# Keys of three heads beside the small columns: summed tile by tile of the tokens, on all eight PSUM banks

## The chip, the cores and the metric

The kernel runs on one core of a Trainium2 chip. The metric is the device time of one execution in microseconds; shown is the median of several runs. The engines are TensorE (PE, matrix products into PSUM), VectorE (DVE), ScalarE (ACT) and GpSimd (POOL); SyncE (SP) issues most of the transfers. PSUM has eight banks of 512 fp32 values on each of 128 partitions.

## The reference, cut to what matters

The block is a hybrid decoder layer on 16 + 512 = 528 tokens of width 1024. Only its head matters for the change:

```python
n = _rmsnorm(h, pre_mix_norm[l])
proj = jnp.einsum('btd,dn->btn', n, w_in[l])
(gq, gk, gv, gz, gb, ga, aq, ak, av, iq, ik, iw, gate_a, gate_b) = jnp.split(proj, split_at, axis=-1)
y_gdn = _gdn_branch(gq, gk, gv, gz, gb, ga, ...)   # causal convolution, silu, gated delta rule
y_dsa = _dsa_branch(aq, ak, av, iq, ik, iw, ...)   # sparse attention
```

`gk` has eight heads of 128 columns. `gb`, `ga`, `ik` and `iw` are 8, 8, 64 and 8 columns, 88 in all; the kernel calls them misc. From `gb` and `ga` come the write strength and the decay of the delta rule, without which its inverse (I + L)^-1 cannot begin.

## The kernel before, in words

Every fp32 product is done in three: an operand is split into a high part (a copy in the matmul's reduced fp32 form) and a low part (the rest), and hi·hi, hi·lo and lo·hi are summed. `wload` loads a chunk of weights (`raw`, 2 buffers), makes `hi` on ACT and `lo` on DVE (`hl`, 5 buffers).

The input comes transposed, as eight tiles of 128 features by 528 tokens. The first loop (lines 131 to 142) loads tile k to `xr`, makes `nhi` on ACT and `nlo` on DVE, squares it and adds the square to `sqs`. The norm itself (one factor per token) is applied after the products, because it commutes with them.

`proj_a` (line 184) multiplies one chunk of weights, held as the stationary operand, with all tokens: two halves of 264 tokens, for each half the eight tiles k, three products each. A chunk is thus 48 products into two PSUM tiles. It is called for misc (88 columns, line 203) and then for each head of the keys (`keys`, line 321), later for values and queries.

`token_scales` (line 144) sums `sqs` over the features with five products by a vector of ones (`ssn`), takes the inverse root (`rn`) and spreads it over the partitions (`rb`, via the matrix `ones` and diagonal matrices). misc is transposed by tokens (`scp`), scaled to `sc`, and yields the decay `gg`, its running sums `gcp` (with the triangle `tri`), and through memory the matrix `E`. `conv` scales a head's columns by `rb` (line 297), convolves them with four taps (ACT line 298, DVE line 301) and applies silu. `key_norms` sums the squares (`kss`), `products` makes L of four heads at a time (`gp`, `lhs`), and 31 steps on DVE (`substitute`) invert its blocks of 32, whose results go to `Y` and into the products `pm`.

PSUM tiles come from two pools: `pp`, 3 banks, for the long sums, and `sp`, 5 banks, for the rest. Buffers named `cv` and `y` (two of each) hold a head's columns, for heads 2, 3, 6 and 7 a wide buffer `tb` (two; the first one holds `tri` and `ones` until `gcp`).

The program's order is not the engines' order: a planner puts each engine's instructions in order from its own estimate of when they are ready, with the program's order as priority; `tc.issue_after(x)` asks that what follows stands behind x on its engine. On the chip each engine then takes its instructions strictly in that order.

Of the kernel before, what the change touches and what calls it, by code (L numbers as in the profile page):

```python
# [10 lines left out]
F32 = mybir.dt.float32  # L11
F32R = mybir.dt.float32r
# [7 lines left out]
P = 128  # L20
# [13 lines left out]
IDX_D = 64  # L34
S4 = {"a": 4 * T, "b": 4 * L}
# [3 lines left out]
def hybrid_block(ctx: ExitStack, tc: tile.TileContext, io: dict):  # L39
# [29 lines left out]
    # ---------------------------------------------------------------- constants  # L69
# [19 lines left out]
    # ---------------------------------------------------------------- weights  # L89
    def wload(src, n, name, spare=False):  # L90
        """one chunk of weights, split; spare: in the buffers tb and st"""
# [11 lines left out]
    def rsqrt(out, a, shape, tag):  # L103
        """out = a ** -0.5 (a > 0): Newton steps from a guess by the exponent"""
# [19 lines left out]
    # ---------------------------------------------------------------- normed activations, transposed and split  # L124
# [5 lines left out]
    sq = [slots.tile([P, 4096], F32, tag=("s5", "s6")[x], name=f"sq{x}")[:, : 4 * T].rearrange("p (k t) -> p k t", t=T) for x in range(2)]  # L130
    for k in range(KT):
        nc.sync.dma_start(xr[:, k, :], io["hT"][:, k, :])
        if k == 0:
            w_misc = wload(io["w_misc"], 8 * 88, "misc")
# [6 lines left out]
        if k:  # L141
            V.tensor_tensor(sqs, sqs if k > 1 else sq[0][:, 0, :], sq[k // 4][:, k % 4, :], ALU.add)

    def token_scales():
        """1 / rms of the tokens: on partitions (rn) and along the free axis on every partition (rb)"""
# [26 lines left out]
    # ---------------------------------------------------------------- dense products, weights stationary  # L172
    marks, todo = [], []

    def later(keep=0, part=None):
        """what the tensor engine does with earlier convolved columns, behind a part of the latest products"""
        while len(todo) > keep:
            if part is None:
                todo.pop(0)()
            else:  # L180
                with tc.issue_after(marks[part].ins):
                    todo.pop(0)()

    def proj_a(w, name, moving=None, m=P, full=True):
        """columns of one weight chunk [P, 8, m] against the tokens: psum parts [(tile, first column, n)]"""
# [14 lines left out]
    # ---------------------------------------------------------------- small columns: index key, beta, decay, index weights  # L200
    misc = const("misc", [96, T])
    G.memset(misc[64:96, :], 0.0)
    for pt, c, n in proj_a(w_misc, "misc", m=88):
        S.copy(misc[:88, c : c + n], pt[:88, :n])
# [36 lines left out]
    # cumulated log decay in each chunk (the 16 leading tokens, then chunks of 128)  # L241
# [16 lines left out]
    # rows of gc, through memory, on every partition  # L258
# [10 lines left out]
    # decay between the tokens of a chunk: E[p, (h j), f] = exp(-|gc_p - gc_f|)  # L269
# [14 lines left out]
    # ---------------------------------------------------------------- causal convolution and silu  # L284
    silu = []

    def conv(g, c0, parts_of, out, name, wide=False):
        """out = silu(conv) of the tokens from c0"""
        if wide:
            both = wk.tile([P, 2, T], F32, tag="tb", name=f"cb_{name}", bufs=2)  # L290
            cv, y = both[:, 0, :], both[:, 1, : T - c0]
        else:
            cv = wk.tile([P, T], F32, tag="cv", name=f"cv_{name}", bufs=2)
            y = wk.tile([P, T], F32, tag="y", name=f"cy_{name}", bufs=2)[:, : T - c0]
# [11 lines left out]
    # ---------------------------------------------------------------- keys of the delta rule  # L306
# [10 lines left out]
    # XL: blocks 0, 1 (and below them) and 2 of the inverse; XL, L1: the blocks of L below the diagonal of 64 and of 32  # L317
# [3 lines left out]
    def keys(h):  # L321
        w = wload(io["w_k"][h], 1024, f"k{h}")
        parts = proj_a(w, f"k{h}")
        later(1, 0)
        sq = conv(8 + h, 0, parts, kT[:, h, :], f"k{h}", wide=h % 4 > 1)
        S.activation(sq, kT[:, h, :], AF.Square)
        todo.append(lambda: key_norms(h, sq))
# [10 lines left out]
    def products(x):  # L338
        """L[c, s] = beta_c r_c^2 (k_c . k_s) E of 4 heads (i = h * 4 + j); its blocks on the diagonal, by memory, to lanes"""
# [23 lines left out]
        # lane = x * 64 + i * 4 + block  # L363
# [20 lines left out]
    # ---------------------------------------------------------------- (I + L)^-1: 32-blocks, one on each lane  # L384
# [5 lines left out]
    def substitute(nlane, n, lt, x, tmp):  # L390
        """x = (I + L)^-1 of the block of each lane, then its transpose in tmp; in steps"""
# [42 lines left out]
    # ---------------------------------------------------------------- values of the delta rule: r beta v, tokens on partitions  # L434
    vb = slots.tile([P, 32, P], F32, tag="s5", name="vb")
    vbm = cst.tile([NM, NH, P], F32, tag="st", name="vbm", bufs=2)
    for h in range(NH):
# [4 lines left out]
        if h == 1:  # L442
# [3 lines left out]
            # upper triangle (with the diagonal) of E for the scores  # L446
# [14 lines left out]
    # ---------------------------------------------------------------- queries; scores against the keys of the chunk  # L461
# [32 lines left out]
    # ---------------------------------------------------------------- dense products, tokens stationary  # L494
    def rows_part(pt, pairs, lhs, t, cs, first=True, last=True):
        """adds to one psum tile the products of some chunks [P, 2, 512], (number, (hi, lo)), for the columns cs"""
# [9 lines left out]
    def proj_half(src, name, lhs, evac):  # L506
        """512 columns for all tokens, chunk by chunk of the weights"""
# [724 lines left out]
```

## Time and profile before

| | us |
|---|---|
| median of 3 runs (lowest, highest) | 1077.09 (1076.67, 1077.24) |
| span of the profiled execution, first to last instruction | 1075.6 |
| what lies around that span, against the median | 1.5 |
| PE busy in the span | 1054.0 |
| PE busy in its first 20 us | 9.95 |

A timeline row reads: start, time, engine, line, operation, output <- inputs, shapes, how many; in brackets, how long the engine had been idle and what ended that. Matmuls are pipelined: their rows overlap, and what one costs is the step from one start to the next. An fp32 product that is not split (of the identity, of keys with keys) appears as two matmul rows.

### The profile page before, as it was taken

The page shows a single profiled execution, that of the slowest core. Times are in us where ns is not written, and L with a number is a line of the kernel's source. Part 1 is how long each engine was busy: PE and PEld are TensorE (multiplying, and loading weights), DVE is VectorE, ACT ScalarE, POOL GpSimd, SP SyncE. Part 2 cuts the span into 40 slices and gives each one's busy share as a digit, 9 for nine tenths or more (in the row PEclk, how much of TensorE's full clock was granted, in tenths as well). Part 3 has the DMA queues.
Part 4 walks back from the last instruction along what each step waited for, and adds up shares of the span by engine and source line. Part 5 has one row for each costly group of instructions (what it writes and reads, how often), then busy time and mean ns, then how long its engine had stood idle before and what let it go on. Part 6 is the DMA issues. An engine that isn't in the chain of part 4 may idle for free.

```text
span 1075.6 us, 15893 instructions
## 1 busy us (share of the span) xinstructions
PE 1054.0 (98%) x6249; PEld 903.8 (84%) x6249; DVE 682.8 (63%) x1502; ACT 461.4 (43%) x854; POOL 61.6 (6%) x85
## 2 busy tenths in 40 slices
PE   6999999999999999999999999999999999999996
PEld 5999999999997678898888888898888888888885
DVE  5797899516689789957867555695442343343346
ACT  5465555444268432235665432473432332232130
POOL 4202302100000000000000000000000000000022
PEclk9999999998999999999999999999999999999999
DMA  5433424210133022232121235332322333333332
GB/s 177 117 102 108 116 82 136 68 41 2 43 101 115 20 79 80 97 99 82 56 59 59 80 90 187 96 95 83 98 88 90 97 98 98 87 90 98 98 98 79
DMA packets 28235, 96.44 MB, mean 90 GB/s; under 512 B 3632, under 2 KB 3968, under 8 KB 28160
## 3 DMA queue, kind: packets, MB, share of 16 engines
q1 hardware_dynamic: 25440, 87.51, 26.1%
q0 software_dynamic: 2720, 7.92, 2.8%
q8 instruction: 49, 0.80, 0.3%
q14 instruction: 26, 0.21, 0.1%
HBM read 90.14 MB, written 5.28 MB: 89 GB/s over the span
## 4 chain that ended last, share of the span: by engine, by line
PE 89%; DVE 6%; DMA 2%; ACT 2%; issue 1%; SPq 0%; DVEq 0%; ACTq 0%
PE up L1102 5%; PE up L1103 5%; PE up L1101 5%; PE d L503 4%; PE d L504 4%; PE d L502 4%; PE pa_dense L889 2%; PE pa_dense L890 2%; PE pa_dense L888 2%; PE pa_bg L194 1%; PE pa_q L195 1%; PE pa_q L193 1%; PE pa_q L194 1%; PE pa_bg L193 1%; PE pa_bg L195 1%; PE bd L1009 1%
## 5 line engine op out<-in xcount | busy, mean ns | idle before, releaser
L1102 PE MATMUL up<-n2l,hi_up 128*128 128x512 f32 (+1 forms) x288 | 106.8, 372 | 0.0
L1101 PE MATMUL up<-n2h,hi_up 128*128 128x512 f32 (+1 forms) x288 | 106.6, 371 | 0.0
L1103 PE MATMUL up<-n2h,lo_up 128*128 128x512 f32 (+1 forms) x288 | 106.6, 371 | 0.0
L100 DVE TENSOR_TENSOR lo_up<-raw_up,hi_up 128x1024 fp32r<-128x1024 f32 x32 | 39.2, 1225 | 71.0 <-PE up L1102 53.0
L100 DVE TENSOR_TENSOR lo_d<-raw_d,hi_d 128x1024 fp32r<-128x1024 f32 x24 | 29.4, 1226 | 78.4 <-PE d L503 56.0
L502 PE MATMUL d<-hi_d,uh 128*128 128x512 f32 x192 | 75.9, 396 | 0.0
L504 PE MATMUL d<-hi_d,ul 128*128 128x512 f32 x192 | 75.9, 395 | 0.0
L503 PE MATMUL d<-lo_d,uh 128*128 128x512 f32 x192 | 75.9, 395 | 0.0
L1102 PEld LDWEIGHTS up<-n2l,hi_up 128*128 128x128 f32 x288 | 54.2, 188 | 10.3
L1101 PEld LDWEIGHTS up<-n2h,hi_up 128*128 128x128 f32 x288 | 54.2, 188 | 10.3
L1103 PEld LDWEIGHTS up<-n2h,lo_up 128*128 128x128 f32 x288 | 54.1, 188 | 10.3
L1105 ACT ACTIVATE rup<-up 128x512 f32<-128x512 f32 (+1 forms) x36 | 19.9, 552 | 99.6 <-PE up L1103 99.6
L99 ACT CAST hi_d<-raw_d 128x1024 fp32r<-128x1024 f32 x24 | 25.2, 1049 | 59.6 <-PE d L504 59.6
L99 ACT CAST hi_up<-raw_up 128x1024 fp32r<-128x1024 f32 x32 | 33.4, 1044 | 24.0 <-PE d L504 22.7
L504 PEld LDWEIGHTS d<-hi_d,ul 128*128 128x128 f32 x192 | 36.1, 188 | 8.7
L502 PEld LDWEIGHTS d<-hi_d,uh 128*128 128x128 f32 x192 | 36.1, 188 | 8.7
L503 PEld LDWEIGHTS d<-lo_d,uh 128*128 128x128 f32 x192 | 36.1, 188 | 8.7
L888 PE MATMUL pa_dense<-nhi,hi_dense 128*128 128x512 f32 x96 | 39.3, 409 | 0.0
L889 PE MATMUL pa_dense<-nlo,hi_dense 128*128 128x512 f32 x96 | 38.0, 396 | 0.0
L890 PE MATMUL pa_dense<-nhi,lo_dense 128*128 128x512 f32 x96 | 38.0, 396 | 0.0
L546 PE MATMUL pb_z<-hi_z,nhi 128*128 128x256 f32 x128 | 37.9, 296 | 0.0
L193 PE MATMUL pa_k<-nhi,hi_k 128*128 128x264 f32 x128 | 37.1, 290 | 0.0
(570 smaller groups left out, 3079.3 us busy)
## 6 DMA issues: line engine op xcount, KB each, us to landing
raw_up<-w_up SPq DMA_DIRECT2D x32, 512.0 KB, 3.6
raw_d<-w_down SPq DMA_DIRECT2D x24, 512.0 KB, 3.6
raw_k<-w_k SPq DMA_DIRECT2D x8, 512.0 KB, 4.1
raw_v<-w_v SPq DMA_DIRECT2D x8, 512.0 KB, 4.2
raw_q<-w_q SPq DMA_DIRECT2D x8, 512.0 KB, 3.5
raw_z<-w_z SPq DMA_DIRECT2D x8, 512.0 KB, 3.6
raw_w_ga<-w_ga SPq DMA_DIRECT2D x8, 512.0 KB, 3.6
raw_bg<-w_bg SPq DMA_DIRECT2D x8, 512.0 KB, 3.6
```

The lines of the kernel that those rows point to most:

```text
L99: S.copy(hi[:, :n], raw[:, :n])
L100: V.tensor_tensor(lo[:, :n], raw[:, :n], f(hi[:, :n]), ALU.subtract)
L193: TE.matmul(pt[:m, :n], hi[:, ws], mh[:, k, ms], start=(k == 0), stop=False)
L502: TE.matmul(pt, lh, whi, start=beg, stop=False)
L503: TE.matmul(pt, lh, wlo, start=False, stop=False)
L504: TE.matmul(pt, ll, whi, start=False, stop=end)
L888: TE.matmul(pt, hi[:, ws], nhi[:, k, NM:], start=(k == 0), stop=False)
L889: TE.matmul(pt, hi[:, ws], nlo[:, k, NM:], start=False, stop=False)
L890: mm = TE.matmul(pt, lo[:, ws], nhi[:, k, NM:], start=False, stop=(k == KT - 1))
L1101: TE.matmul(pt, hi[:, ws], n2h[:, k, ms], start=(k == 0), stop=False)
L1102: TE.matmul(pt, hi[:, ws], n2l[:, k, ms], start=False, stop=False)
L1103: TE.matmul(pt, lo[:, ws], n2h[:, k, ms], start=False, stop=(k == KT - 1))
```

## The change

The eight tiles are still loaded in order, but the weights of misc and of key heads 0, 1 and 2 now come with them, for two tiles at a time (944 columns: 2 x 88 and 3 x 2 x 128), and each tile's products go at once into eight PSUM tiles that stay open over all k: misc, k0, k1, k2, two halves each. Ahead of them stand 20 products of the identity with itself, into a bank that the sums later overwrite. After the eighth tile the sums are copied to SBUF, and `keys` of heads 0 to 2 starts from these copies. Comments are dropped; nothing else differs.

```diff
+NHEAD = 3
+    heads = [(88 * 2 * (i > 0) + 256 * max(i - 1, 0), 88 if i == 0 else P) for i in range(NHEAD + 1)]
+    hps = [[ptile(f"hd{i}{x}", pp if i > 1 and i + x != 4 else sp) for x in range(2)] for i in range(NHEAD + 1)]
+    for _ in range(20):
+        warm = TE.matmul(hps[NHEAD][1][:, :P], ident, ident, start=True, stop=True)
+    def head_weights(k):
+        n = 2 * 88 + 256 * NHEAD
+        raw = wp.tile([P, 1024], F32, tag="raw", name=f"raw_head{k}", bufs=2)
+        nc.sync.dma_start(raw[:, : 2 * 88], io["w_misc"][:, k * 88 : (k + 2) * 88])
+        nc.sync.dma_start(raw[:, 2 * 88 : n].rearrange("p (h c) -> p h c", h=NHEAD), io["w_k"][:NHEAD, :, k * P : (k + 2) * P].rearrange("h p c -> p h c"))
+        hi, lo = (wp.tile([P, 1024], F32R, tag="hl", name=f"{x}_head{k}", bufs=5) for x in ("hi", "lo"))
+        S.copy(hi[:, :n], raw[:, :n])
+        V.tensor_tensor(lo[:, :n], raw[:, :n], f(hi[:, :n]), ALU.subtract)
+        return hi, lo
     for k in range(KT):
         nc.sync.dma_start(xr[:, k, :], io["hT"][:, k, :])
-        if k == 0:
-            w_misc = wload(io["w_misc"], 8 * 88, "misc")
+        if k % 2 == 0:
+            hw = head_weights(k)
...
+        for (o, m), pts in zip(heads, hps):
+            ws = slice(o + k % 2 * m, o + k % 2 * m + m)
+            for x in range(2):
+                ms = slice(x * HT, x * HT + HT)
+                with tc.issue_after(warm.ins):
+                    TE.matmul(pts[x][:m, :HT], hw[0][:, ws], nhi[:, k, ms], start=(k == 0), stop=False)
+                    TE.matmul(pts[x][:m, :HT], hw[0][:, ws], nlo[:, k, ms], start=False, stop=False)
+                    TE.matmul(pts[x][:m, :HT], hw[1][:, ws], nhi[:, k, ms], start=False, stop=(k == KT - 1))
...
-    for pt, c, n in proj_a(w_misc, "misc", m=88):
-        S.copy(misc[:88, c : c + n], pt[:88, :n])
+    for x in range(2):
+        S.copy(misc[:88, x * HT : x * HT + HT], hps[0][x][:88, :HT])
+    headc = []
+    for i in range(NHEAD):
+        headc.append(conv_columns(f"k{i}", wide=i % 4 > 1))
+        for x in range(2):
+            (S.copy if x else V.tensor_copy)(headc[i][0][:, x * HT : x * HT + HT], hps[1 + i][x][:, :HT])
...
     def keys(h):
-        w = wload(io["w_k"][h], 1024, f"k{h}")
-        parts = proj_a(w, f"k{h}")
-        later(1, 0)
-        sq = conv(8 + h, 0, parts, kT[:, h, :], f"k{h}", wide=h % 4 > 1)
+        if h < NHEAD:
+            sq = conv(8 + h, 0, [], kT[:, h, :], f"k{h}", columns=headc[h])
+        else:
+            parts = proj_a(wload(io["w_k"][h], 1024, f"k{h}"), f"k{h}")
+            later(1, 0)
+            sq = conv(8 + h, 0, parts, kT[:, h, :], f"k{h}", wide=h % 4 > 1)
         S.activation(sq, kT[:, h, :], AF.Square)
         todo.append(lambda: key_norms(h, sq))
```

`conv_columns` is the allocation of `cv` and `y` (or the wide buffer), taken out of `conv`; `HT` is 264, `KT` 8.

## Rows read from the trace of the kernel before

**Rows 1.** The page's first part: the span, and PE's busy time, share and instructions.
```profile
span 1075.6 us, 15893 instructions
PE 1054.0 (98%) x6249; PEld 903.8 (84%) x6249; DVE 682.8 (63%) x1502; ACT 461.4 (43%) x854; POOL 61.6 (6%) x85
```

**Rows 2.** The waits of PE over the whole span: waiting line, whom it waited for, us in total, times, longest.
```profile
PE pa_misc L193 <- ACT hi_misc L99: 6.6, 1, 6.6
PE pa_misc L193 <- ACT nhi L135: 2.4, 1, 2.4
PE pa_misc L194 <- DVE nlo L136: 1.0, 1, 1.0
PE vtp L453 <- ACT cy_v L303: 0.9, 1, 0.9
PE vtp L453 <- DVE lhs L360: 0.8, 1, 0.8
```

**Rows 3.** Stretches of the span: length, busy time of PE, PEld, DVE, ACT, POOL, then granted clock, DMA share and GB/s.
```profile
0.00:20.00 20.00, 9.95 (x50) 8.86 (x50) 11.42 (x15) 11.37 (x19) 11.79 (x26) 1.00 0.58 185
9.00:13.00 4.00, 1.59 (x6) 1.25 (x6) 2.62 (x2) 3.38 (x6) 2.40 (x3) 1.00 1.04 407
29.85:83.80 53.95, 53.79 (x441) 51.88 (x440) 45.24 (x108) 29.00 (x63) 7.57 (x11) 1.00 0.41 118
83.80:121.90 38.10, 36.45 (x314) 35.52 (x313) 29.38 (x75) 22.47 (x47) 14.48 (x14) 1.00 0.44 123
```

**Rows 4.** The timeline of PE at the start, matmuls only.
```profile
11.93 0.52 PE L194 MATMUL pa_misc<-nlo,hi_misc 128*88 128x264 f32 x1 [1.00 <-DVE nlo L136]
...
16.82 0.42 PE L193 MATMUL pa_misc<-nhi,hi_misc 128*88 128x264 f32 x1
17.04 0.42 PE L195 MATMUL pa_misc<-nhi,lo_misc 128*88 128x264 f32 x1
...
17.62 0.28 PE L195 MATMUL pa_misc<-nhi,lo_misc 128*88 128x264 f32 x1
...
26.41 0.28 PE L193 MATMUL pa_k<-nhi,hi_k 128*128 128x264 f32 x1
...
30.07 0.29 PE L193 MATMUL pa_k<-nhi,hi_k 128*128 128x264 f32 x1
```

**Rows 5.** PE's groups by form from 0 to 43.3 us: line, operation, shapes, count | busy us, mean ns | idle before.
```profile
L193 PE MATMUL pa_k<-nhi,hi_k 128*128 128x264 f32 x49 | 14.4, 294 | 0.0
...
L164 PE MATMUL pb<-dg,tri 128*128 128x128 f32 x8 | 1.6, 290 | 0.0
L152 PE MATMUL ssn<-one,sqs 128*128 128x1 f32 x8 | 1.1, 253 | 0.0
L208 PE MATMUL scp<-ident,misc 32*128 32x32 f32 x4 | 0.6, 233 | 0.0
L246 PE MATMUL gcp<-gg,tri 128*128 128x32 f32 x2 | 0.4, 286 | 0.0
L244 PE MATMUL gcp<-gg,tri 128*128 128x32 f32 x2 | 0.4, 286 | 0.1
...
```

**Rows 6.** The timelines of ACT and DVE at the start.
```profile
5.73 0.78 ACT L99 CAST hi_misc<-raw_misc 128x704 fp32r<-128x704 f32 x1
9.62 0.73 ACT L135 ACTIVATE nhi<-xr,gT 128x528 fp32r<-128x528 f32 x1 [3.11 <-DMA xr<-hT]
24.18 0.38 ACT L296 COPY cv_k<-pa_k 128x264 f32<-128x264 f32 x1 [2.75 <-PE pa_k L195]
...
10.38 5.02 DVE L136 SCALAR_TENSOR_TENSOR nlo<-xr,gT,nhi 128x528 fp32r<-128x528 f32 x5 [2.95 <-ACT nhi L135]
18.54 1.22 DVE L100 TENSOR_TENSOR lo_k<-raw_k,hi_k 128x1024 fp32r<-128x1024 f32 x1
22.60 2.19 DVE L142 TENSOR_TENSOR sqs<-sqs,sq 128x528 f32<-128x528 f32 x3
```

**Rows 7.** The timeline of POOL: the identity is made; the eight transfers to `E` are issued.
```profile
1.22 0.29 POOL L72 TENSOR_SCALAR_AFFINE_SELECT ident<-ident 128x128 f32<-128x128 f32 x1
...
44.67 6.01 POOL L272 DMA_DIRECT2D E<-gcd x8 [2.19 <-DMA gcd<-gts]
```

**Rows 8.** Transfers issued from 0 to 130 us: out<-in, queue, count, KB each, median us from issue to landing.
```profile
xr<-hT SPq DMA_DIRECT2D x8, 264.0 KB, 7.6
E<-gcd POOLq DMA_DIRECT2D x8, 256.0 KB, 6.7
raw_misc<-w_misc SPq DMA_DIRECT2D x1, 352.0 KB, 4.0
```

**Rows 9.** The timelines of PE and DVE: the token scales and the running sums of the decay.
```profile
25.16 1.19 PE L152 MATMUL ssn<-one,sqs 128*16 128x1 f32 x10
29.68 0.17 DVE L116 SCALAR_TENSOR_TENSOR rn<-t_n,y_n 128x5 f32<-128x5 f32 x1
39.13 0.20 PE L247 MATMUL gcp<-gg,tri 16*16 16x8 f32 x2
```

**Rows 10.** The chain that ended last, from 0 to 210 us: products of keys with keys, 16 of them in 32 matmuls.
```profile
79.50 3.68 PE gp L358 x32
```

**Rows 11.** The timelines of POOL and PE: the last transfer into Y, and the first product that reads Y.
```profile
191.09 0.65 POOL L417 DMA_DIRECT2D Yb<-yd  x1
210.69 2.11 PE L582 MATMUL pm<-Ya,lam 32*32 32x32 f32 x64
```

More of the change, by code (lines that the diff above doesn't have):

```diff
@@ L198, in proj_a, with conv_columns @@
         return parts
+    def conv_columns(name, wide=False):
+        if wide:
+            both = wk.tile([P, 2, T], F32, tag="tb", name=f"cb_{name}", bufs=2)
+            return both[:, 0, :], both[:, 1, :]
+        return [wk.tile([P, T], F32, tag=x, name=f"{x}_{name}", bufs=2) for x in ("cv", "y")]
     misc = const("misc", [96, T])
     G.memset(misc[64:96, :], 0.0)
-    for pt, c, n in proj_a(w_misc, "misc", m=88):
-        S.copy(misc[:88, c : c + n], pt[:88, :n])
+    for x in range(2):
[5 more added lines that the diff above has]
+            (S.copy if x else V.tensor_copy)(headc[i][0][:, x * HT : x * HT + HT], hps[1 + i][x][:, :HT])
     scp = stile("scp")
@@ L285, in hybrid_block, with conv @@
     silu = []
[L287 to L294, printed above, removed]
+    def conv(g, c0, parts_of, out, name, wide=False, columns=None):
+        cv, y = columns or conv_columns(name, wide)
+        y = y[:, : T - c0]
         for pt, c, n in parts_of:
```

## The prediction

> **What bounds the kernel now.** I read the page's first part first: PE is busy 1054.0 of 1075.6 us [rows 1], so only time in which PE stands or runs slowly can be won. PE's waits come next [rows 2]: of 11.7 us in the five rows, 10.0 lie in the products of misc, at the very start; the other two, 0.9 and 0.8 us at the transposes of the values (`vtp`), are the next place where PE stands. The stretches agree: in the first 20 us PE is busy 9.95 [rows 3]. Then the timeline of PE, for what "busy" hides [rows 4]: consecutive misc products start 0.22 us apart at 16.82 and 17.04, while key products of the same length take 30 steps from 26.41 to 30.07, 0.122 us each; the row at 17.62 already has the shorter duration (0.28 against 0.42). Half the pace: PE ran at the lower of its two levels (1.2 GHz) until about 17.5 us and at 2.4 GHz from there. The granted-clock column reads 1.00 for the whole stretch [rows 3], so here I go by the steps. Before the rise PE had worked without a long pause from 11.93.
>
> How much is lost? Misc and heads 0 to 2 are 4 x 48 = 192 products. Up to 43.3 us the grouped view counts 49 of each of the three key products, 147 in all, 144 of which belong to heads 0 to 2 [rows 5]; so these 192 end at about 43.2. At the fast pace they are 192 x 0.122 = 23.4 us. In the same stretch PE also does the small work: the five groups shown after the keys are 4.1 us busy [rows 5], seven still smaller ones of 0.2 to 0.4 bring them to 5.8, and since neighbours overlap I take 5.3. Lost: 43.2 - 23.4 - 5.3 = 14.5 us. A later start of PE's useful work, or a shorter one, moves the end one for one, as long as PE is kept fed later.
>
> **The change part by part.**
>
> *The identity products.* 20 fp32 products are 40 matmuls. At the fast level such a matmul costs 3.68 / 32 = 0.115 us [rows 10]; slow I scale by 0.22 / 0.122 to 0.21. The identity is finished at 1.22 + 0.29 = 1.5 us [rows 7], so they run from about 1.6. All fast would end at 6.2, all slow at 10.0. Between the two I take 27 slow and 13 fast, 1.6 + 5.7 + 1.5 = 8.8: nearer to all slow, because the misc products after a rest were slow for most of their run [rows 4]. PE has nothing else to do until 6.6 [rows 2], so the first 5 us cost nothing.
>
> *The first weights.* One load of 352 KB took 4.0 us to land [rows 8]; now it is 472 KB in two transfers: scaled, 5.4 us from an issue at 1.7, 7.1, and the cast (944 columns against 704 in 0.78 us [rows 6], 1.0) gives 8.1, hidden behind the identity products. If it takes the 7.6 us of the tokens' tiles [rows 8], it lands at 9.3 and PE starts at 10.3, 1.5 us later. So PE starts at 8.8, bounds 8.1 and 10.3.
>
> *Keeping PE fed.* A tile now brings 24 products, 2.9 us fast. Tile 1 was split at 9.62 [rows 6]; with more ahead of it I allow 11. PE reaches it at 8.8 + 2.9 = 11.7. Bytes are the same as before, 4 x 472 = 352 + 3 x 512 KB. The new pieces are shorter (704 and 1024 bytes a row), which no load of [rows 8] shows as such. The nearest are the eight transfers to `E`, rows of 512 bytes: 2.1 MB issued over 6.0 us [rows 7], the last landing some 6.7 later [rows 8], about 165 GB/s; the loads of 9 to 13 us move 407 GB/s [rows 3]. At those ends all tiles and weights, 4.1 MB, are in by 27 and by 12 us; the last tile is needed at 8.8 + 7 x 2.9 = 29. On SP the loads of tiles 5 to 7 now stand behind two loads that wait for a `raw` buffer, freed when the first and second `lo` are made, about 9.5 and 14: no one is late by that. ACT and DVE cast as many columns as before (3776), only earlier: 1.0 and 1.1 us four times. DVE's list until the last `nlo` is 8 x 1.0 + 4 x 1.1 [rows 6], 12.4, with the adds of `sqs` (0.73 each) 17.5: done at 24 at the latest, before PE needs it. Cost nothing, and 2 to 3 us if PE has to wait for each of the first tiles.
>
> *The end of the sums.* 8.8 + 23.4 = 32.2 us. Lost is then 8.8 instead of 14.5: **gain 5.7 us**; with the bounds of the start 4.2 to 6.4.
>
> *The copies out.* All eight banks are open, so nothing else on PE can run until one is copied. Misc is summed first within a tile, and its copies (0.38 [rows 6]) are done while the heads' last products run; the first `pp` bank is free some 0.5 us after its last product, while the last bank is still summed. Nothing, at most 1 us. Under Matmuls, "Perfetto Trace Analysis" of the Trainium skill says independent groups should rotate through different banks, so that copying one out overlaps the next group's products. By that rule this change gives up the overlap; the trace has no stretch with eight banks open that could show its price.
>
> *What becomes late.* `ssn` needs a bank of `sp`, and those five are held until the misc copies at about 30.5 (29.2 for the last tile's start, 0.7 of misc, a copy). It ran at 25.16 and will run at 31 to 33. `rn` followed its start by 4.5 us, 1.2 of it another head's `lo`; it was ready at 29.85 and is now at 34.4 to 36, so 4.6 to 6.1 us later, and `rb`, `gcp` [rows 9], `E` and the inverse with it. Heads 0 to 2 wait in SBUF for `rb`. Head 3's wide buffer is the one that holds `tri` until `gcp`, which goes from 39 to about 44; PE then has three `pp` banks for heads 3 and 4, and head 4's second half comes due at 45: 0 to 1.5 us. DVE worked 45.2 of 53.95 us from `rn` to the end of the keys' convolutions (83.8) [rows 3]. Two `lo` (2.4 us [rows 6]) are now made before `rn`, leaving 42.8. Without a pause it ends at 77.2, with half of its old 8.7 us of pauses, from 34.4, at 81.6: 2.2 us earlier than before, where PE is 5.7 earlier. The difference, 3.5, must come out of the 8.7 us in which DVE stood from 83.8 to 121.9 [rows 3]. I let two thirds come out of there, and PE loses **1.2**. Bounds: 0, and all 5.7 if that chain does not move. Farther on there is room: the last transfer to `Y` is issued at 191.1 and, even at the 6.7 us of `E` [rows 8], has landed by 198; PE reads it at 210.7 [rows 11].
>
> *Sum.* 5.7 - 1.2 = 4.5 us. The profiled span of 1075.6 becomes 1071.1; with the 1.5 us around it, and against the median of 1077.1, **1072.6**.
>
> **The rivals.**
>
> *The gain stops at the values.* PE comes early to a DVE that is hardly earlier: the waits for `vtp` [rows 2] grow by 3 to 5 us. For it: DVE already sets the `vtp` waits. Against: PE could work ahead, there is buffer room for two heads. Net gain 1 to 3: about 1075. If the whole gain goes so, 1077.
>
> *Slow and starved at the start.* If PE waits a little for each tile, it may stay at 1.2 GHz until the last tile is in, about 18 us. From 8.8 that is 42 slow products; the other 150 need 18.3 us: 36.3 instead of 32.2, gain 1.6, 1075.5. For it: exactly this happened to misc from 11.93 to 17.5 [rows 4]. Against: a tile now brings four times the products, so PE is late, not the tile. "TensorE: Matmul & The Clock Gate" of the Trainium skill, in "Loop structure matters more than you think", warns of this very loop, a transfer waited for ahead of each product, and says the clock falls; the misc rows here agree with it.
>
> *Slower: the scales.* `rn` comes 4.6 to 6.1 us late, and 2.4 us of DVE's work is out of the way. If DVE recovers nothing of its 17.4 us of pauses up to 121.9, the chain into `vtp` comes 2.2 to 3.7 us later than today, and PE with it: about 1080. It decides from the point where DVE recovers less than that; above it there is a gain.
>
> *The planner finds a better order.* The two `vtp` waits go and nothing is given back: 1077.1 - 5.7 - 1.7 = 1069.7.
>
> **How the numbers follow.** About 0.2% (2.15 us) is what a measurement of this kernel can tell from no change. Forecast (1070.8 to 1074.0) 0.55; gain mostly stopped at the values 0.17; slow start 0.08; all given back, about 1077, 0.08; slower 0.07; better than 6.5 us 0.05. Faster than 1074.9: 0.55 + 0.05 + 0.11 + 0.04, about 0.76; same 0.16; slower 0.08. The range from 1069.4 to 1076.4 leaves out the slower case, the whole give-back and little more, under 0.2.
>
> **What the new profile would show.** Right: PE busy with the identity from 1.6 to about 9; the step of 264-column products 0.12 us from the first head product on, or soon after; the last head product at 31 to 33.5; `ssn` behind it, `rn` at 34 to 37; head 3 without a pause of over 1 us; waits of PE after 32 us below 3 us. Wrong: steps of 0.22 us beyond 14 us; a last head product after 35; PE waiting for over 4 us in total between 32 and 130, at a copy out of PSUM, at `kss` or at `vtp`. What would upset the forecast most is a new order of the planner far behind the change.

## The result: slower by 14.5 us, 14.2 of it before the first product that reads `Y`

| | before | after |
|---|---|---|
| time, median of the runs | 1077.16 us | 1091.66 us |
| ratio, 95% interval | | 1.0119 [1.0075, 1.0162] |
| profiled span, mean granted clock of PE | 1075.6 us, 0.995 | 1090.2 us, 0.984 |

The change makes the kernel slower (the medians by 1.3%, the ratio of the runs by 1.2%), and the forecast of 1072.6 us (range 1069.4 to 1076.4) has the wrong sign. Where the time goes is quickly found: the first product that reads `Y` started at 210.69 us [rows 11]. The timeline of PE has it now at:

```profile
224.90 2.11 PE L619 MATMUL pm<-Ya,lam 32*32 32x32 f32 x64
```

That is 14.2 us later; the spans differ by 14.6, so little is added after it. Single executions of one kernel can be some 15 us above its median, with a granted clock of 0.50 in a stretch far behind `pm` (380 to 400 us in the profiled ones of n2 and blate2 below, 1104.75 and 1101.85 us), so the experiments' profiles are read only up to `pm`. The waits of PE over the whole span after the change (line waiting, whom it waited for, us in total, times, longest) answer to [rows 2]:

```profile
PE pa_k L220 <- ACT hi_k L100: 3.5, 1, 3.5
PE kss L370 <- ACT y_k L363: 3.1, 1, 3.1
PE hd L138 <- POOL ident L73: 1.6, 1, 1.6
PE hd L167 <- ACT hi_head L146: 1.5, 1, 1.5
PE pa_k L222 <- DVE lo_k L101: 1.5, 1, 1.5
PE pa_k L220 <- ACT cv_k L331: 1.4, 1, 1.4
...
PE hd L169 <- DVE lo_head L147: 0.7, 1, 0.7
```

The waits at the start are shorter (1.6 + 1.5 + 0.7 against 10.0), but four new ones lie among the keys: 3.5 + 3.1 + 1.5 + 1.4 = 9.5 us, where the kernel before had none. The stretches of the changed kernel (length, busy time of PE, PEld, DVE, ACT and POOL, granted clock, DMA share, GB/s) show what comes with them:

```profile
0.00:20.00 20.00, 16.23 (x109) 15.80 (x110) 11.71 (x15) 12.77 (x20) 11.99 (x26) 0.91 0.67 209
20.00:40.00 20.00, 20.00 (x169) 19.74 (x168) 11.09 (x30) 5.80 (x10) 1.30 (x2) 1.00 0.35 109
40.00:60.00 20.00, 15.47 (x112) 14.13 (x110) 14.67 (x45) 9.84 (x22) 5.65 (x9) 0.89 0.14 18
60.00:80.00 20.00, 14.98 (x80) 14.19 (x80) 13.06 (x23) 8.05 (x19) 1.93 (x3) 0.67 0.40 119
...
56.70:69.30 12.60, 12.53 (x59) 12.01 (x60) 5.24 (x9) 5.56 (x16) 5.23 (x8) 0.50 0.80 209
76.00:80.00 4.00, 1.98 (x7) 1.69 (x8) 4.00 (x7) 1.14 (x3) 0.00 (x0) 0.52 0.11 17
80.00:84.00 4.00, 4.00 (x24) 4.00 (x23) 4.00 (x8) 1.45 (x2) 0.00 (x0) 0.62 0.51 170
```

Of the kernel before, the two middle stretches were:

```profile
40.00:60.00 20.00, 20.00 (x166) 19.27 (x165) 12.85 (x23) 10.91 (x24) 7.57 (x11) 1.00 0.68 187
60.00:80.00 20.00, 20.00 (x168) 19.52 (x166) 19.27 (x37) 12.32 (x29) 0.00 (x0) 1.00 0.24 79
```

Up to 40 us PE is better off than before: 16.23 us busy instead of 9.95 in the first 20 [rows 3]. From 40 to 80 it is busy 30.4 us instead of 40, and part of these run at the lower level: the granted clock is 0.50 (1.2 GHz) from 56.7 to 69.3, and near that again from 76 to 83. "Busy" hides that half again, as it did at the start of the kernel before; here the clock column shows it. What the front won and the keys lost must give the 14.2: in the prediction's own count, 192 products now end at 35.05 and need 23.4, so 11.7 us are lost in the front, against 14.5: 2.9 won. The keys have then lost 14.2 + 2.9 = 17.1: 9.5 of standing and, by subtraction, some 7.6 of slow running behind it. The clock column gives about the same: of the 12.5, 2.0 and 4.0 us that PE was busy in the last three stretches, the part that the clock withheld comes to some 8.7.

Why PE stands shows in the order of time. The timelines of PE, DVE and ACT along the path from the sums to `kss` of head 0:

```profile
35.53 1.18 PE L179 MATMUL ssn<-one,sqs 128*16 128x1 f32 x10
...
39.02 0.17 DVE L117 SCALAR_TENSOR_TENSOR rn<-t_n,y_n 128x5 f32<-128x5 f32 x1
...
42.87 0.59 ACT L195 COPY rb<-pb 128x512 f32<-128x512 f32 x1 [1.14 <-PE pb L191]
...
50.36 0.19 DVE L278 SCALAR_TENSOR_TENSOR gg<-gg,ea 128x40 f32<-128x40 f32 x1
...
51.49 0.20 PE L286 MATMUL gcp<-gg,tri 16*16 16x8 f32 x2
...
53.46 0.24 ACT L296 ACTIVATE kts<-kts 128x40 f32<-128x40 f32 x1
53.71 1.28 ACT L338 ACT_TABLE_LOAD   x1
55.00 1.18 ACT L338 ACTIVATE kT<-y_k 128x528 f32<-128x528 f32 x2
56.09 1.16 ACT L363 ACTIVATE y_k<-kT 128x528 f32<-128x528 f32 x2
...
56.77 2.01 PE L370 MATMUL kss<-one,y_k 128*16 128x1 f32 x10 [3.14 <-ACT y_k L363]
```

`ssn` and `rn` are 10.4 and 9.3 us later than before [rows 9]. From `rn` to `gg` DVE needs 11.3 us: the scaling of three heads by `rb` and their taps became due at once and stand between the steps of the decay. `gcp` is 12.4 us late [rows 9]: 9.3 come with `rn`, and 3.0 more because the way from `rn` to `gcp` grew from 9.5 to 12.5. On ACT every silu is queued behind the last exponential of that chain, so head 0's silu runs at 55.0, its square at 56.1; and PE's queue has head 0's `kss` ahead of further products of head 5. (These would have stood as well: DVE splits head 5's weights at 55.07, until 56.3.) The second group of stops, farther on, in the same three timelines:

```profile
55.07 1.21 DVE L101 TENSOR_TENSOR lo_k<-raw_k,hi_k 128x1024 fp32r<-128x1024 f32 x1
61.28 0.69 DVE L320 TENSOR_TENSOR E<-E,gc 128x512 f32<-128x512 f32 x1 [5.01 <-DMA E<-gcd]
77.33 1.22 DVE L101 TENSOR_TENSOR lo_k<-raw_k,hi_k 128x1024 fp32r<-128x1024 f32 x1
...
61.40 0.17 ACT L372 COPY ssk<-kss 128x4 f32<-128x4 f32 x1 [1.83 <-PE kss L370]
...
64.65 0.17 ACT L372 COPY ssk<-kss 128x4 f32<-128x4 f32 x1 [2.40 <-PE kss L370]
...
75.46 1.03 ACT L100 CAST hi_k<-raw_k 128x1024 fp32r<-128x1024 f32 x1
...
76.54 0.59 PE L220 MATMUL pa_k<-nhi,hi_k 128*128 128x264 f32 x1 [3.54 <-ACT hi_k L100]
78.60 0.59 PE L222 MATMUL pa_k<-nhi,lo_k 128*128 128x264 f32 x1 [1.47 <-DVE lo_k L101]
```

DVE splits head 5's weights at 55.07 and head 6's at 77.33. Between them lie 5.0 us in which it stands at the first slice of `E`, and convolutions that come late. They come late because ACT, which starts each of them, has to copy out the sums of `kss` first and waits for PE, which makes them at half pace: 1.8 and 2.4 us at 61.40 and 64.65. So the first stop feeds the second. PE wants heads 6 and 7 before that.

### The profile page after: what moved, and what is told of

Same layout as the page of the kernel before. It is cut to its first block, busy times and chain, and to the rows that moved or that the text cites. A ratio compares the mean times of both kernels' runs of the same rounds, so it can differ in the third digit from the quotient of the medians.

```text
span 1090.2 us, 15987 instructions
## 1 busy us (share of the span) xinstructions
PE 1065.6 (98%) x6289; PEld 916.0 (84%) x6289; DVE 686.4 (63%) x1505; ACT 461.9 (42%) x851; POOL 61.9 (6%) x85
## 4 chain that ended last, share of the span: by engine, by line
PE 88%; DVE 6%; ACT 3%; DMA 2%; issue 1%; SPq 0%; DVEq 0%; ACTq 0%
PE up L1140 5%; PE up L1139 5%; PE up L1138 5%; PE d L540 4%; PE d L541 4%; PE d L539 4%; PE pa_dense L926 2%; PE pa_dense L927 2%; PE pa_dense L925 2%; PE pb_z L583 1%; PE pa_bg L221 1%; PE pa_q L222 1%; PE pa_q L220 1%; PE pa_q L221 1%; PE pa_bg L220 1%; PE pa_bg L222 1%
## 5 line engine op out<-in xcount | busy, mean ns | idle before, releaser
L1139 PEld LDWEIGHTS up<-n2l,hi_up 128*128 128x128 f32 x288 | 54.2, 188 | 10.3
L1138 PEld LDWEIGHTS up<-n2h,hi_up 128*128 128x128 f32 x288 | 54.2, 188 | 10.3
L1140 PEld LDWEIGHTS up<-n2h,lo_up 128*128 128x128 f32 x288 | 54.1, 188 | 10.3
L100 ACT CAST hi_up<-raw_up 128x1024 fp32r<-128x1024 f32 x32 | 33.5, 1046 | 24.4 <-PE d L541 22.7
L220 PE MATMUL pa_v<-nhi,hi_v 128*128 128x264 f32 x128 | 37.1, 290 | 0.0
```

Of the source, the lines that this page charges most:

```text
L100: S.copy(hi[:, :n], raw[:, :n])
L220: TE.matmul(pt[:m, :n], hi[:, ws], mh[:, k, ms], start=(k == 0), stop=False)
L1138: TE.matmul(pt, hi[:, ws], n2h[:, k, ms], start=(k == 0), stop=False)
L1139: TE.matmul(pt, hi[:, ws], n2l[:, k, ms], start=False, stop=False)
L1140: TE.matmul(pt, lo[:, ws], n2h[:, k, ms], start=False, stop=(k == KT - 1))
```

## Experiments

My theory was that late scales alone do this. The rivals: three heads that arrive together fill ACT and DVE whenever the scales come; DVE's stop at the transfer of `E`; the splits of late heads queued too low; the identity products. The table gives, from each profiled execution, the start of `ssn`, of the last `gcp` and of the first `pm`, then the median time and the ratio's interval against the kernel before on the same chip. For several kernels the median lies 3 to 5 us farther above that of the kernel before than `pm` is late (n2, blate2, misc2, misc3, bwarm); the experiments do not explain that part.

| kernel | ssn | gcp | pm | median | interval |
|---|---|---|---|---|---|
| before | 25.16 | 39.13 | 210.69 | 1077.16 | |
| changed | 35.53 | 51.49 | 224.90 | 1091.66 | 1.0075 to 1.0162 |
| blate1 | 25.42 | 40.20 | 208.14 | 1077.07 | 0.9973 to 1.0045 |
| blate2 | 30.03 | 46.50 | 218.16 | 1088.09 | 1.0080 to 1.0172 |
| blate | 37.73 | 53.76 | 226.26 | 1094.10 | 1.0082 to 1.0183 |
| n1 | 30.56 | 45.34 | 214.38 | 1082.62 | 1.0037 to 1.0111 |
| n2 | 33.36 | 49.76 | 220.56 | 1090.22 | 1.0062 to 1.0208 |
| scales0 | none | 40.37 | 218.10 | 1087.01 | 1.0033 to 1.0105 |
| selate | none | 41.51 | 215.97 | 1083.67 | 1.0046 to 1.0085 |
| misc1 | 22.71 | 44.71 | 221.26 | 1087.69 | 1.0059 to 1.0122 |
| misc2 | 30.74 | 48.15 | 219.03 | 1090.02 | 1.0088 to 1.0124 |
| misc3 | 29.88 | 44.52 | 217.37 | 1088.96 | 1.0067 to 1.0138 |
| edec | 36.24 | 52.20 | 220.81 | 1088.54 | 1.0087 to 1.0118 |
| aelate | 36.05 | 52.00 | 221.60 | 1088.64 | 1.0090 to 1.0119 |
| wahead | 35.27 | 51.22 | 221.68 | 1095.75 | 1.0155 to 1.0221 |
| silufree | 35.89 | 51.98 | 224.50 | 1093.72 | 1.0083 to 1.0211 |
| nowarm | 35.58 | 51.49 | 224.07 | 1091.40 | 1.0059 to 1.0169 |
| bwarm | 21.67 | 34.66 | 212.48 | 1081.44 | 1.0027 to 1.0079 |
| n1f | 24.88 | 44.08 | 214.47 | 1082.28 | 1.0041 to 1.0087 |
| n1g | 24.38 | 40.79 | 209.56 | 1078.52 | 0.9989 to 1.0041 |

### Late scales alone: blate, blate2, blate1

The products of the kernel before, chunk by chunk from loads of their own; `ssn` is held on PE behind the products of three, two or one head. These heads' products and copies are also written ahead of the scales and the decay chain, as in the changed kernel. The number of heads (`NHEAD`) is all that differs between the three.

```diff
-        if k % 2 == 0:
-            hw = head_weights(k)
+        if k == 0:
+            w_misc = wload(io["w_misc"], 8 * 88, "misc")
...
+        for pt, c, n in proj_a(wload(io["w_k"][i], 1024, f"k{i}"), f"k{i}"):
+            S.copy(headc[i][0][:, c : c + n], pt[:, :n])
...
+            with tc.issue_after(marks[-1].ins):
                 TE.matmul(ssn[:n, t : t + 1], sqs[:, c : c + n], one, start=True, stop=True)
```

> The converse: the order of the kernel before (small columns alone as the tokens land, then the heads one by one with their own loads of 512 KB, no identity products), but the ssn products are queued on PE behind the products of the first three heads, so that the scales come about as late as in the changed kernel. Theory (late scales): ssn near 32, rn near 36, gcp 46 to 50, E 57 to 60; PE then stops at kss and at late splits as in the changed kernel, time 1084 to 1092. Rival (three heads arriving together): here they arrive 4 us apart, time 1077 to 1081.

> blate with the ssn products held behind the products of the first head only: ssn near 28, rn near 32 (before 25.2 and 29.7), gcp 42 to 44. If the loss grows in step with the lateness (blate: 12.6 us later ssn, 15.6 us lost): 3 us later cost 3 to 4.5 us, time 1080 to 1082. If there is slack first (the chain of waits before shows no stop of PE at the scales): 1076.5 to 1078.5.

> blate with the ssn products held behind the products of the first two heads: ssn near 31, rn near 35, gcp 45 to 48, between blate1 (25.4; no loss) and blate (37.7; 17 us lost). Loss in step with the lateness: about half, 1083 to 1088. Threshold above this (slack of 6 us or more): 1076 to 1079.

PE's waits in blate:

```profile
PE pa_k L195 <- ACT hi_k L100: 3.5, 1, 3.5
PE kss L345 <- ACT y_k L338: 3.1, 1, 3.1
...
PE pa_k L195 <- ACT cv_k L306: 1.5, 1, 1.5
PE pa_k L197 <- DVE lo_k L101: 1.5, 1, 1.5
```

These are the four stops of the changed kernel, to a tenth of a microsecond, without an identity product, a short load or a head summed beside another. With `ssn` at 25.42 (blate1) none of them is left and the time is that of the kernel before. So late scales are enough to bring the four stops about, with the three heads coming one after the other; their convolutions still come due together (`rb` is applied at 45.8, 46.5 and 47.2), because all wait for `rb`. (That the heads are written ahead of the decay chain goes with it: for one head, in blate1, it costs nothing; for three it was not tried with early scales. Held behind three heads `ssn` came 6 us later than I had said, and blate ends 2 us above its range; blate1 became a control, for its `ssn` is as early as before; blate2 lies at the upper end of its range.) There is no slack of 4.6 us: that much lateness (blate1 to blate2) put `pm` 10.0 us back, the next 7.7 another 8.1. Whether the first microsecond or two are free these runs do not tell. blate2's stop is a different one (the timeline of PE):

```profile
71.92 0.59 PE L195 MATMUL pa_k<-nhi,hi_k 128*128 128x264 f32 x1 [5.63 <-ACT hi_k L100]
```

so which instruction PE stands at depends on the order; that it stands does not.

### Fewer heads: n2, n1

```diff
-NHEAD = 3
+NHEAD = 2
```

(and 1).

> The changed kernel with two heads summed together with the small columns in place of three. Theory: 48 fewer products ahead of ssn (48 x 0.122 = 5.9 us at the fast step), so ssn near 30.5 instead of 35.5 and rn near 34; fewer convolutions wait for rb; time 1078 to 1086. Rival (burst of heads, scales of no account): the same direction, two convolutions at once instead of three, 1080 to 1086. Rival (the front alone is worth what was forecast and something far behind spoils it): no change against three heads, 1090 to 1093.

> The changed kernel with one head summed together with the small columns. Theory: ssn near 25 to 27 since PE then follows the tokens' arrival, rn near 30, E as in the kernel before; time 1072 to 1078. Rival (burst of heads): also near the kernel before, 1074 to 1079. Rival (the stop at E or the identity products cost the time): 1085 to 1092 as with three heads.

`ssn` came 3 us later than said for n2, and 4 to 5 later for n1. `pm` follows it down: 224.90, 220.56, 214.38. The times of both missed the theory's ranges, and n2's 1090.22 lies in the range of the last rival, "no change"; its `pm` is 4.3 us earlier than in the changed kernel all the same. In n2 PE stood 4.2 us at a split of the head weights and 6.8 at a split among the keys, and hardly at `kss` (0.3). In n1 the front has a wait of its own, 6.0 us at a split of the head weights. The timelines of ACT (the cast) and DVE (the split, two of them):

```profile
12.39 0.54 ACT L146 CAST hi_head<-raw_head 128x432 fp32r<-128x432 f32 x1
...
21.38 1.12 DVE L147 TENSOR_TENSOR lo_head<-raw_head,hi_head 128x432 fp32r<-128x432 f32 x2
```

The halves were there at 12.9; DVE's order put the split behind the last tokens and sums of squares.

### Three heads together, scales early: scales0, selate

```diff
-        V.tensor_scalar(rn_a[:, 1:5], ssn[:, 1:5], 1.0 / D, EPS, ALU.mult, ALU.add)
+        V.tensor_scalar(rn_a[:, 1:5], sq[0][:, 0, 1:5], 1.0 / D, EPS, ALU.mult, ALU.add)
...
-            S.copy(rb[:, NM:], pb)
+            S.copy(rb, sq[0][:, 0, :])
```

selate moves `decay_abs` and the subtraction in `zsp` behind the keys' loop and head 6's split:

```diff
+    with tc.issue_after(split_done["k6"].ins):
+        for h in range(NH):
+            decay_abs(h)
```

> The changed kernel with the scales taken from data that lies ready early, so that they no longer depend on the summed products: scp, ssn, pc and pb are left out; rn is worked out from five columns of the first squared tile, sc from a slice of the first tile of tokens, and rb is a copy of that squared tile (so the numbers that come out are others; the decay chain, the convolutions, E and all else stay). The three heads still arrive together at 35 us. Theory (the late scales are the cause): gcp near 36 and E near 47 in place of 51.5 and 61.3, kss without a stop, waits of PE from 36 to 100 us below 3 us, time 1069 to 1076. Rival (three heads arriving together fill ACT and DVE whenever the scales come): PE still loses 6 us or more from 36 to 100, time 1081 to 1090.

> scales0 (the changed kernel with scales taken from early data, scp, ssn, pc and pb left out), and besides DVE's work on the transferred E and zsp is queued behind the split of the weights of k6. If DVE's stops at these transfers (2.4 and 5.0 us in scales0) make the rest of the loss: kss of the third head without its stop of 3.7 us, first gp products 4 us or more earlier than in scales0, time 1078 to 1083. If the three heads arriving together make it: 1085 to 1089 as in scales0.

scales0 speaks for the rival: its time, 1087.01, lies in the range of "three heads arriving together", and PE's waits from 36 to 100 us, 5.2, lie between the two forecasts (below 3, and 6 or more). It is not a clean test, for `gcp` came at 40.37, not 36. PE waited 3.9 us for a split of head weights at 26.6, because the steps of `rn` had been placed ahead of it on DVE, and 3.7 at `kss`. DVE stood at a transfer before that:

```profile
61.07 0.28 DVE L296 TENSOR_TENSOR zsp<-zsp,gc 16x128 f32<-16x128 f32 x1 [4.96 <-DMA zsp<-gcdm]
```

Early scales bring `pm` from 14.2 us late to 7.4; with the work on `E` moved it is 5.3 (selate, whose median is 3.3 us lower, between its two forecasts). These 5.3 are left. The front is part of them: the sums end at 39.7 in scales0 and at 40.8 in selate, against 35.05 in the changed kernel. On the other side both leave out PE's products for the scales (`scp`, `ssn`, `pb`, about 3.3 us busy in [rows 5]). So there is a rest among the keys, and three heads that arrive together may make it; these runs do not tell it apart. Late scales are enough for the four stops and for a loss of nearly this size (blate's `pm` is 15.6 us late); that they are all of the changed kernel's loss is not shown.

### Scales forward, three heads kept: misc1, misc2, misc3

misc1 sums the small columns from a load of their own, ahead of all heads. misc2 lets them go first in the last three tiles; misc3 in the last four, with the decay chain written ahead of the last sums:

```diff
-        for (o, m), pts in zip(heads, hps):
+        sums(k, range(1 if k > 4 else NHEAD + 1))
...
+    for k in (5, 6):
+        sums(k, range(1, NHEAD + 1))
+    last_pb = scale_rows()
+    sums(7, range(1, NHEAD + 1), last_pb)
```

> The changed kernel, but the small columns have their own load of weights again and their products, copies, transposes and the five ssn products stand ahead of the products of the three heads; the identity products and the three heads summed together stay. Theory (the scales are late because the small columns end with the heads, and the late scales bring the three convolutions and the decay chain onto DVE at once): ssn near 25, rn near 30, rb near 34, PE waits between 40 and 85 us below 4 us (9.5 us in the changed kernel), no 1.2 GHz stretch after 50 us, time 1070 to 1079. Rival (three heads arriving together are the load, whenever the scales come): waits at hi and lo weights of k5 to k7 and at kss remain, time 1085 to 1092. Rival (DVE stopped by the transfer of E): E comes about 11 us earlier, so the stop at E goes too; this run alone does not part it from the theory, edec does.

> The changed kernel with the same loads, identity products and three heads, but in the last three tiles of tokens the small columns' products go first; scp and ssn stand in PE's queue ahead of the heads' products of tiles 5 to 7, and pb and pc (the rows of rn) ahead of those of tile 7. Theory (late scales): ssn at 24 to 27, rn at 28 to 31, rb at 32 to 36, gcp at 37 to 41, E at 48 to 52, the front as good as in the changed kernel (PE 4 us ahead of the kernel before at 35 us), waits of PE between 40 and 100 us below 3 us: time 1071 to 1077. Rival (three heads that arrive together fill ACT and DVE whenever the scales come): kss and lo_k still stop PE for 5 us or more, time 1083 to 1092.

> As misc2, but the small columns go first from tile 4 on (not from tile 5), and the decay chain is written down ahead of the heads' last products and the copies of the heads out of PSUM, so that it stands ahead of the convolutions on DVE. Theory (late scales): ssn 25 to 27, gcp 36 to 40, E 46 to 50, front as in the changed kernel: 1071 to 1078. Rival (burst of heads): 1083 to 1090.

All three missed the theory's ranges, and their times, 1087.69, 1090.02 and 1088.96, lie in those of the rival. `gcp` says why none is the clean test I took it for: the scales were not early. In misc1 `ssn` ran at 22.71, but `pb` stood behind all heads on PE (43.7), so `rb` came at 47.6, later than in the changed kernel; and starved of tokens its products ran at half pace from 12.4 to 21.7. In misc2 `ssn` was at 30.74: when the last tokens had landed (21.07) PE was at the third of the eight tiles, and it came to the small columns of the last three at 27.17. misc3 has `gcp` at 44.52; its `pm` is 6.7 us late, its median 11.0 us above that of the kernel before on its chip.

### Links of the path: silufree, edec, aelate, wahead

```diff
-        with tc.issue_after(last_exp.ins):
+        with (tc.issue_after(last_exp.ins) if columns is None else ExitStack()):
             silu.append(
```

silufree, above, frees the silu of heads 0 to 2. edec moves the loop of `decay_abs` behind the keys; aelate is the changed kernel with selate's move; wahead asks for each head's weights one head earlier.

> The changed kernel without the rule that the silu of the first three heads stands behind the last exponential of the decay chain on ACT. It tests the path from the late scales to kss: gcp (51.5), its exponentials, the first silu, its square, kss of k0 (56.8, PE stops 3.1 us). Theory in this form: the stop at kss goes, k0's kss comes up to 5 us earlier, time 1086 to 1090. Rival (DVE full with three convolutions is what makes kss late, not that rule): no change within 2 us, 1090 to 1093.

> The changed kernel with the decay preparation of all eight heads (the subtraction on the transferred E and its absolute value on DVE) put behind the loop over the keys in place of between heads 4 to 7. Theory (the late scales pile up the convolutions): the stops of PE at the copy out of PSUM (48.6) and at kss of k0 (56.8) stay, since both lie ahead of E's arrival at 61.3; DVE's 5.0 us idle at E goes, so the waits at hi and lo of k6 and k7 (5.0 us) shrink in part; time 1085 to 1090. Rival (DVE's stop at E's transfer is the cause): those 5 us and the slow clock behind them go, time 1079 to 1085. Rival (E is needed soon, its late preparation costs behind the keys): slower than 1091.7.

> The changed kernel with DVE's work on the transferred E and zsp queued behind the split of the weights of k6; the scales stay late. If DVE's stop at E (5.0 us) is a link of the loss: the stops at hi_k of k7 (3.5) and lo_k of k6 (1.5) and part of the slow stretch behind them go, time 1082 to 1087. If the late scales work through gcp, silu and kss alone: the stops ahead of 61 us (cv_k 1.4, kss 3.1) stay and time is 1088 to 1092.

> The changed kernel with the weights of each key head asked for one head earlier, so that their split stands earlier in the queues of ACT and DVE; nothing else. Rival (the splits of k5 to k7 stand too low in the queues): waits at hi_k and lo_k between 70 and 85 us go (5.0 us, and the slow clock around them), time 1082 to 1087. Theory (late scales): convolutions and splits share the same DVE that is full from 43 to 56 us; an earlier split delays kss instead; time within 3 us of 1091.7.

silufree took the stop at `kss` away and got others: 3.2 at a copy out, 2.5 and 2.6 at splits; its time is above both forecasts. edec did not do what it was made for: `E`'s first slice stayed where it was, with 5.3 us of standing; the splits came earlier (heads 6 and 7 at 68.5 and 71.1 instead of 77.3 and 81.0), and 3 us were won. In aelate DVE no longer stood at `E`, but 6.0 us at the next instruction, a tap that waits for ACT's part of that convolution; the splits came at 69.4 and 71.8. The stops at heads 6 and 7 went, those at `cv_k` (1.4) and `kss` (3.1) stayed, and 1.5 and 1.3 came at the values; 3.0 us in the median. So the stop at `E` by itself costs nothing that these runs show, since another of its length lies under it; what both runs won must come from the work on `E` that no longer stands ahead of two splits. wahead moved the stops as well (2.1 at a split, 1.2 at a later `kss`); its runs spread from 1089.52 to 1101.45, and I draw nothing from their median. Cutting one link gives back 3 us at best; the queue stops at the next.

### The identity products: nowarm, bwarm

nowarm is the changed kernel without them, bwarm the kernel before with them, into a PSUM tile that nothing reads.

```diff
-    for _ in range(20):
-        warm = TE.matmul(hps[NHEAD][1][:, :P], ident, ident, start=True, stop=True)
```

> The changed kernel without the 20 products of the identity. Theory: the first head products run at the 0.22 us step for longer, ssn 1 to 4 us later than 35.5, time 1091 to 1096. Rival (the identity products cost time: they hold PE or bring the fall of the clock at 11.4 us): ssn at 34 to 35.5, time 1088 to 1091.

> The kernel before with the 20 products of the identity alone added, in a PSUM tile that nothing reads. In the kernel before 18 products of the small columns run at the 0.22 us step. If the identity products keep the clock up: those run at 0.12 us, 1 to 2 us less on PE, and since the tokens bound that stretch, time 1075 to 1077. If they do nothing: 1076.5 to 1077.5. If they cost: above 1078.

They win nothing: 1091.40 without, 1091.66 with. Alone, in the kernel before, they cost 0.5%, though `ssn` came 3.5 us earlier; early scales do not help there because the front got worse: the tokens bound it, the misc products ran at half pace from 13.8 to 20.2, and the last ended at 21.4 instead of 19.8 (`pm` is 1.8 us late). The start of PE in the changed kernel shows one reason why they are useless there (timelines of PE and ACT):

```profile
1.57 6.12 PE L138 MATMUL hd<-ident 128*128 128x128 f32 x40 [1.57 <-POOL ident L73]
9.19 0.36 PE L167 MATMUL hd<-nhi,hi_head 128*88 128x264 f32 x1 [1.50 <-ACT hi_head L146]
...
10.37 0.35 PE L169 MATMUL hd<-nhi,lo_head 128*88 128x264 f32 x1 [0.70 <-DVE lo_head L147]
...
11.28 0.37 PE L167 MATMUL hd<-nhi,hi_head 128*128 128x264 f32 x1
11.45 0.42 PE L168 MATMUL hd<-nlo,hi_head 128*128 128x264 f32 x1
...
14.53 0.39 PE L167 MATMUL hd<-nhi,hi_head 128*88 128x264 f32 x1
14.75 0.29 PE L168 MATMUL hd<-nlo,hi_head 128*88 128x264 f32 x1
...
8.16 0.98 ACT L146 CAST hi_head<-raw_head 128x944 fp32r<-128x944 f32 x1 [3.08 <-DMA raw_head<-w_k]
```

They end at 7.7, PE stands 1.5 and 0.7 us, and after a few fast products 14 run at half pace. In nowarm half pace lasts from 9.7 to 14.0, and at 20 us both are at the same product, within one.

### A version without late scales: n1f, n1g

One head beside the small columns, and DVE's order mended: each split ahead of the tokens' tile that needs it. n1f also put the later splits behind `rn`; n1g takes that back for head 1 and keeps head 2's cast behind the copies of the small columns.

```diff
+        with (tc.issue_after(halved[k // 2].ins) if k % 2 else ExitStack()):
             V.scalar_tensor_tensor(nlo[:, k, :], xr[:, k, :], gT[:, k : k + 1], f(nhi[:, k, :]), ALU.mult, ALU.subtract)
```

> The changed kernel with one head summed with the small columns (n1), and DVE's order mended: each split of the head weights stands ahead of the second token tile that needs it and of the sums of squares (in n1 PE waits 6.0 us for a split that DVE reaches at 21.4, though its halves were there at 12.9), and the splits of the later heads stand behind rn. Theory: the wait of 6.0 us goes, ssn 25 to 28 in place of 30.6, rn 29 to 32, nothing lost in the keys: 3 to 6 us less than n1, time 1075 to 1079. Rival (the identity and the small loads cost it): 1080 to 1083.

> n1f, but the split of head 1's weights no longer stands behind rn (in n1f PE waited 2.8 us for it at 29.7), and the cast of head 2's weights stands behind the copies of the small columns on ACT. Theory: ssn 24 to 27, rn 28 to 30, gcp 39 to 42, PE's loss up to 35 us 2 us below that of the kernel before, nothing lost in the keys: time 1073 to 1077. Rival (one head with the small columns costs 4 us by itself, as in n1 and n1f): 1080 to 1083.

n1f had `ssn` at 24.88, but PE then waited 2.8 us for head 1's split, and `gcp` was at 44.08. n1g has `ssn` at 24.38, `gcp` at 40.79 and no stop among the keys. `pm` is 1.1 us earlier than before, and the time, outside both ranges, cannot be told from that of the kernel before. So there is no version here that beats it. (n1f's time lies in its rival's range.)

## Why the prediction was wrong

**What bounds the kernel.** Right: PE's idle or slow time is what counts, and 14.5 us of it lay in the front.

**Identity products, first weights.** 8.8 forecast, 7.7 measured; the first head product at 9.19, inside 8.1 to 10.3.

**Keeping PE fed, the end of the sums.** Forecast 32.2, bounds 31 to 33.5; measured 35.05. The tokens were in time, as argued. The three terms that are short: 0.4 for the start, 0.8 for the wait for the first `lo_head`, 1.5 for the slow stretch. The rival "slow and starved", at 36.3, had the half pace but not its reason: no product waited for a tile, and this is not the loop with a wait for a transfer ahead of each product. Gain 2.9 in place of 5.7.

**The copies out** cost nothing, as said: `scp` starts at 35.15, behind the last sum. The rule on rotating banks (Matmuls, "Perfetto Trace Analysis" of the Trainium skill) has no price in this trace: with all eight banks open, the next work on PE began 0.2 us after the start of the last sum's last product.

**What becomes late.** This is the step that failed. The times were short first: `ssn` 35.5 instead of 31 to 33, `rn` 39.0 instead of 34.4 to 36, `gcp` 51.5 instead of 44; 3.0 of these last 7.5 us because I kept the old distance from `rn`, though three heads would be waiting for `rb` beside the decay chain. But the size of the error is in the method. I set DVE's work (42.8 us) against its pauses and looked for the result at `vtp`, as if any work could fill any pause. The queues work in order. PE stood at the instructions whose input was late, first for 1.4 us at a copy out, then for 3.1 at `kss`, reached through `gcp`, the exponentials, silu and square, a path that was written in the code and that I read only for `rb`. The step's 1.2 us (bounds 0 to 5.7) became 17.1: 9.5 of standing, the rest the lower clock, which had no term among the keys at all. blate, with late scales and the front of the kernel before, has the same four stops and a `pm` that is 15.6 us late; what of the 17.1 the three heads' arrival adds is open. I had also given head 3's wide buffer 0 to 1.5 us; PE's stop at `cv_k` of 1.4 is of that size. Head 3's sums did wait for `gcp` (copied out at 51.73); the stop ended before that, when DVE was through with head 0's taps at 48.05 and ACT copied head 4's first half (48.16) into the buffer of head 0.

**The rivals.** "Slower: the scales" named the cause, with the wrong place (`vtp`, where waits fell to 0.7 and 0.4) and the wrong price (3 us), and a chance of 0.07. The signs of failure that I listed came true: steps of 0.22 us beyond 14 us, a last head product after 35 (barely: it ends at 35.05), over 4 us of waits, at `kss` and at a copy out.

## What to carry to other kernels

When a change makes a value late, do not divide work by time on the engine that recovers it: walk from that value through every queue to the first instruction on the bounding engine that needs it, and ask what stands behind that instruction. Work that is summed "with" other work ends with it, so put what others wait for first. And a stop on PE can cost more than its length: here 9.5 us of standing in four stops brought a further 7.6 us lost at half pace, though the first, 1.4 us at 48.6, brought none (the granted clock is 1.00 from 48.5 to 53.6).

## What the runs showed of the hardware

A stop of 3.1 us, in the middle of a stretch that had been busy, was followed by a granted clock of 0.50 for 12.6 us (56.7 to 69.3) in which PE was busy 12.53 us. The ten matmuls of one `kss` took 2.01 us there (56.77, 59.36, 62.60) and 1.18 afterwards (71.82). The clock column does not always tell. A stretch of the changed kernel, and one of nowarm:

```profile
11.30:14.70 3.40, 3.40 (x18) 3.40 (x17) 3.40 (x4) 3.11 (x7) 1.83 (x3) 0.51 0.92 288
```

```profile
9.60:14.00 4.40, 4.33 (x19) 4.24 (x20) 4.34 (x4) 4.40 (x8) 2.64 (x3) 1.00 0.77 243
```

Both have steps of 0.22 us; the column reads 0.51 in the one, where PE had worked before, and 1.00 in the other, where it had not. "TensorE: Matmul & The Clock Gate" of the Trainium skill, in "Loop structure matters more than you think", warns that a long wait for a transfer ahead of every product drops the clock. No loop here is quite that. The nearest is misc1: after waits of 2.0 and 1.5 us for the tokens the steps are 0.22 us from 12.4 to 21.7 (granted clock 0.50), with one more wait, of 0.8 us, among them.
